# A decoder layer at one sequence of 256 tokens on one NeuronCore: four loads of x, modulation four k tiles ahead, later multiplies by the norm factor, and x1 scaled before it is transposed

## The chip, the cores and the metric

The kernel runs on one core of a Trainium2 chip. The metric is the device time of one execution in microseconds (us). The core has five engines that run side by side, each through its own instructions in its own order: PE (matrix products; PEld in the profile is its weight load), DVE (element-wise work), ACT (activation functions, with a scale and a bias per partition), POOL (hardly used here) and SP (issues most of the DMA transfers). An instruction that needs something from another engine or from a transfer waits at a semaphore, and everything queued behind it on its own engine waits with it.

## What is computed

One layer of a conditioned decoder, all in float32, for 256 tokens of 2048 channels:

```python
mod = silu(c) @ w_ada + b_ada        # shift1, scale1, gate1, shift2, scale2, gate2
h   = rms_norm(x, g_norm1) * (1 + scale1) + shift1
p   = h @ w_in                       # retention and HGRN2 inputs, and two branch gates
...                                  # yA, yB: the two attention-like branches
x   = x + gate1 * ((sigmoid(gA) * yA + sigmoid(gB) * yB) @ w_out)
h2  = rms_norm(x, g_norm2) * (1 + scale2) + shift2
u   = causal_depthwise_conv3(h2 @ w_up)
a, b = split(u)
x   = x + gate2 * ((silu(a) * b) @ w_down)
out = rms_norm(x, g_final)
```

The two places that the change touches are the two norms with their modulation: the one of x at the very start, and the one of x1 (x after the first branch) ahead of the product with w_up, called "up" below.

## The kernel before

**Products.** Every weight is read once, in pieces of 512 KB (128 partitions by 1024 float32 values, two k tiles of 128 rows by 512 columns). A float32 product is made of three products of rounded parts: ACT copies a piece to a rounded high part `wh` (line 165), DVE subtracts that from the piece to give the low part `wl` (line 170), and PE multiplies high by high, high by low and low by high (lines 187 to 189 with tokens as output rows, 200 to 202 and 913/915 with channels as output rows). There are 12 buffers for raw pieces and 4 each for `wh` and `wl`. The activations are split in the same way into the two halves of a tile (`hT` for the first norm, `h2T` for the second).

**Vectors of the conditioning.** The shift, scale and gate vectors come from w_ada by dot products on DVE (line 380, 1.2 us each, four per k tile of a scale and shift pair).

**The start.** `norm_x` loads x transposed (`xT`, four tiles of four k tiles each) in eight DMAs, squares each half tile (two on DVE, six on ACT), and adds the squares on DVE. `token_rstd` lets PE sum them over the partitions (line 290, 24 instruction records) and spreads the norm factor of each token over all partitions, `rx`. DVE multiplies x by it (`times`, line 370): the first two k tiles one by one from PSUM, and the other fourteen in seven multiplies of two k tiles from a copy `rx_sb`, which a dependence only holds behind the first weight split. `modulated` then writes the high part of `hT` and a full copy `h` on ACT (lines 341, 342), and DVE subtracts (343). Four output groups g = 0 to 3 are started with the first two k tiles; the next groups (g = 4, 5, 6, ...) follow, and a pacing helper interleaves the further dot products. A group's result is copied out of PSUM by ACT (line 691, tiles `p`).

**The x1 to up boundary.** x1 is kept with tokens on the partitions (tiles `xr`, four of 512 channels). The last quarter of the w_out product holds its last k tiles back so that the two token halves t = 0, 1 end apart. For each t, DVE forms gate times product and adds it to x1 (lines 879, 880), ACT squares and sums (882), and ACT and DVE make the norm factor `r` and from it a diagonal matrix `diag` (842). `turn_rows` (line 350) multiplies x1 by `diag` on PE, which transposes and scales it in one step, into a PSUM tile `po` that holds a pair of k tiles. `modulated2` turns each such pair into an `h2T` tile: ACT writes the high part of k tile 0 (line 359), a full copy `h` of k tile 0 (363) and the high part of k tile 1 (359); DVE makes the full copy of k tile 1 from PSUM (361); then DVE makes both low parts (365). `act2(k)` calls this two k tiles ahead of the product that is written next. Three pairs are transposed ahead of the first up product; the pairs 3 to 7 are transposed between up products. One piece of w_up is split ahead of the residual of the last quarter.

**Order.** In this stretch `pin` keeps every engine in the order in which the code is written. Elsewhere it is free where `self.ordered` is false, apart from the manual dependences.

## Time and profile before

| | |
|---|---|
| median of 3 runs | 1540.42 us (1540.33 to 1541.73) |
| the profiled execution | 1540.23 us |
| its span, first to last instruction | 1538.3 us |
| busy: PE, PEld | 1516.6 us (99%), 1308.0 us (85%) |
| busy: DVE, ACT | 1173.4 us (76%), 843.4 us (55%) |
| mean granted TensorE clock | 0.999 |
| read from HBM | 382.11 MB, 250 GB/s over the span |

The rows of a timeline give the start, the duration from first start to last end, the engine, the line, the operation, output and input tiles, and in brackets how long the engine was idle before it and what ended that. An instruction's duration includes a tail that overlaps the next one on the same engine: successive starts on ACT and DVE are some 0.1 us closer than the durations say. Most float32 products on PE have durations of about 0.4 us and start 0.23 us apart. The waits view adds up such idle times by the line that waited and the line that ended the wait.

### The profile page before, as it was taken

The numbers are of one execution on the slowest core, as the hardware profiler recorded it, in microseconds if no ns is written. First come the engines' busy times: TensorE is split into PE (matmuls) and PEld (weight loads), VectorE is DVE, ScalarE is ACT, GpSimd is POOL, SyncE is SP. The second block draws the span as 40 slices with busy tenths as digits, with TensorE's granted clock in tenths as the row PEclk, the third lists the DMA queues.
The fourth block names the chain that finished last, engine by engine and source line by source line (L and its number), as shares of the span: only waits on it lengthen the run. The fifth ranks groups of instructions, "written<-read, shape, count | busy, mean of one in ns | idle before, by whom it ended". The sixth has DMA issues, their size and how long they took to land.

```text
span 1538.3 us, 22200 instructions
## 1 busy us (share of the span) xinstructions
PE 1516.6 (99%) x8286; PEld 1308.0 (85%) x8286; DVE 1173.4 (76%) x1595; ACT 843.4 (55%) x1201; POOL 4.0 (0%) x8
## 2 busy tenths in 40 slices
PE   7999999999999999999999999999999999999997
PEld 6999999888888888888878888888888888888886
DVE  7899986897998977898757787777778769455454
ACT  5755454766865554445446555555555558444343
POOL 0000000000000000000000000000000000000000
PEclk9999999999999999999999999999999999999999
DMA  9999997687777789989946777777777766677651
GB/s 362 346 345 329 319 330 228 232 280 256 247 246 261 262 293 322 320 303 342 337 121 216 226 232 233 240 222 239 230 231 232 226 189 190 206 207 206 198 166 55
DMA packets 111568, 385.69 MB, mean 251 GB/s; under 512 B 12866, under 2 KB 13410, under 8 KB 111460
## 3 DMA queue, kind: packets, MB, share of 16 engines
q1 hardware_dynamic: 110592, 383.14, 76.0%
q8 instruction: 65, 1.06, 0.3%
q10 hardware_dynamic: 868, 1.13, 0.2%
q14 instruction: 43, 0.35, 0.1%
HBM read 382.11 MB, written 2.11 MB: 250 GB/s over the span
## 4 chain that ended last, share of the span: by engine, by line
PE 94%; DVE 3%; ACT 2%; DMA 1%; issue 1%; DVEq 0%; ACTq 0%
PE pg L188 13%; PE pg L187 13%; PE pg L189 13%; PE po L913 11%; PE pg L913 10%; PE po L915 5%; PE pg L915 5%; PE po L189 3%; PE po L188 3%; PE po L187 3%; PE pg L202 3%; PE pg L200 3%; PE pg L201 3%; PE po L556 1%; DVE raw L380 1%; PE po L200 1%
## 5 line engine op out<-in xcount | busy, mean ns | idle before, releaser
L170 DVE TENSOR_TENSOR wl<-raw,wh 128x1024 fp32r<-128x1024 f32 (+1 forms) x536 | 635.0, 1189 | 283.3 <-ACT wh L165 281.9
L165 ACT ACTIVATE wh<-raw 128x1024 fp32r<-128x1024 f32 (+1 forms) x536 | 550.9, 1033 | 529.9 <-PE pg L189 190.4
L380 DVE SCALAR_TENSOR_TENSOR raw<-raw,sc 128x1024 f32<-128x1024 f32 x192 | 233.2, 1217 | 0.0
L913 PE MATMUL pg<-h2T,wh 128*128 128x512 f32 x704 | 221.6, 396 | 1.7 <-DVE h2T L365 1.7
L913 PE MATMUL po<-h2T,wh 128*128 128x512 f32 x704 | 221.2, 395 | 0.2 <-ACT wh L165 0.2
L187 PE MATMUL pg<-wh,hT 128*128 128x512 f32 x512 | 202.6, 396 | 0.0
L188 PE MATMUL pg<-wl,hT 128*128 128x512 f32 x512 | 200.2, 391 | 0.7 <-DVE wl L170 0.7
L189 PE MATMUL pg<-wh,hT 128*128 128x512 f32 x512 | 199.8, 390 | 0.0
L915 PEld LDWEIGHTS pg<-h2T,wl 128*128 128x128 f32 x704 | 131.9, 188 | 31.7 <-DVE wl L170 0.8
L915 PEld LDWEIGHTS po<-h2T,wl 128*128 128x128 f32 x704 | 132.2, 188 | 31.1
L915 PE MATMUL pg<-h2T,wl 128*128 128x256 f32 x704 | 138.5, 278 | 0.0
L915 PE MATMUL po<-h2T,wl 128*128 128x256 f32 x704 | 138.3, 278 | 0.0
L188 PEld LDWEIGHTS pg<-wl,hT 128*128 128x128 f32 x512 | 96.3, 188 | 21.1 <-DVE wl L170 2.3
L189 PEld LDWEIGHTS pg<-wh,hT 128*128 128x128 f32 x512 | 96.1, 188 | 20.2
L187 PEld LDWEIGHTS pg<-wh,hT 128*128 128x128 f32 x512 | 96.2, 188 | 19.1
L202 PE MATMUL pg<-hT,wl 128*128 128x256 f32 x384 | 109.0, 284 | 0.8 <-DVE wl L170 0.8
L200 PE MATMUL pg<-hT,wh 128*128 128x256 f32 x384 | 109.3, 285 | 0.1
L201 PE MATMUL pg<-hT,wh 128*128 128x256 f32 x384 | 109.0, 284 | 0.0
L913 PEld LDWEIGHTS pg<-h2T,wh 128*128 128x128 f32 x704 | 107.2, 189 | 1.8 <-ACT h L363 1.8
L913 PEld LDWEIGHTS po<-h2T,wh 128*128 128x128 f32 x704 | 107.2, 189 | 0.7 <-ACT wh L165 0.6
L200 PEld LDWEIGHTS pg<-hT,wh 128*128 128x128 f32 x384 | 74.1, 193 | 0.9 <-ACT wh L165 0.6
L202 PEld LDWEIGHTS pg<-hT,wl 128*128 128x128 f32 x384 | 74.0, 193 | 1.0 <-DVE wl L170 1.0
(222 smaller groups left out, 2198.4 us busy)
## 6 DMA issues: line engine op xcount, KB each, us to landing
raw<-in_wup SPq DMA_DIRECT2D x176, 512.0 KB, 4.5
raw<-in_wdown SPq DMA_DIRECT2D x88, 512.0 KB, 3.6
raw<-in_wa SPq DMA_DIRECT2D x80, 512.0 KB, 5.6
raw<-in_ada SPq DMA_DIRECT2D x64, 512.5 KB, 5.6
raw<-in_ada SPq DMA_DIRECT2D x64, 512.0 KB, 5.7
raw<-in_wab SPq DMA_DIRECT2D x64, 512.0 KB, 4.8
raw<-in_gate SPq DMA_DIRECT2D x32, 512.5 KB, 4.9
raw<-in_wb SPq DMA_DIRECT2D x32, 512.0 KB, 5.2
```

Source lines behind the costliest of these rows:

```text
L165: self.pin(self.nc.scalar.activation(wh, raw, AF.Copy))
L170: self.last = self.nc.vector.tensor_tensor(wl, raw, wh.bitcast(F32), ALU.subtract)
L187: nc.tensor.matmul(ps[t], lhsT=hi, rhs=wh, start=first, stop=False)
L188: nc.tensor.matmul(ps[t], lhsT=hi, rhs=wl, start=False, stop=False)
L189: nc.tensor.matmul(ps[t], lhsT=lo, rhs=wh, start=False, stop=last)
L200: nc.tensor.matmul(out, lhsT=wh[:, cs], rhs=hi, start=opens, stop=False, skip_group_check=True)
L201: nc.tensor.matmul(out, lhsT=wh[:, cs], rhs=lo, start=False, stop=False, skip_group_check=True)
L202: nc.tensor.matmul(out, lhsT=wl[:, cs], rhs=hi, start=False, stop=last, skip_group_check=True)
L380: dot = self.pin(nc.vector.scalar_tensor_tensor(raw[:, 0, :], raw[:, 0, :], 1.0, self.sc[:, u * GW : u * GW + w], ALU.mult, ALU.mult, accu ...
L556: nc.tensor.matmul(ps[:, j * 64 : (j + 1) * 64], lhsT=(kt if n > 1 else k)[:, h, c * P : (c + 1) * P], rhs=eq[:, j * 64 : (j + 1) * 64], s ...
L913: self.pin(nc.tensor.matmul(ps[j + z], lhsT=wh[:, cs[z]], rhs=act, start=kt == 0, stop=False))
L915: nc.tensor.matmul(ps[j + z][:, :T], lhsT=wl[:, cs[z]], rhs=act[:, :T], start=False, stop=kt == KT - 1)
```

## The change

At the start, x is loaded in four DMAs, each tile is squared at once (one on DVE, three on ACT), the sums are folded to one k tile's width ahead of PE, and the multiplies of later k tiles by `rx_sb` move from "just after the first weight split" to the front of the generator of their own k tiles, held behind the weight split that was traced last. `modulated` makes the full copy of k tile 0 on DVE. At the boundary, `act2` works four k tiles ahead where it worked two, two pieces of w_up are split ahead of the residual where there was one, `modulated2` makes the full copy of the first k tile on DVE and of the second on ACT, with each low part right behind its full copy, and the pairs 3 to 7 are no longer transposed by a product with `diag`: `turn_scaled` multiplies x1 by the norm factor on DVE with tokens on the partitions (tile `xs`) and lets PE transpose that.

```diff
--- before.py
+++ after.py
@@ -268,9 +268,8 @@
     def load_x(self):
 
         out = [self.blk([P, 4, T], name="xT") for _ in range(4)]
-        for i in range(8):
-            u = slice(i % 2 * 2, i % 2 * 2 + 2)
-            self.pin(self.nc.sync.dma_start(out=out[i // 2][:, u, :], in_=self.a["xT"][:, 2 * i : 2 * i + 2, :]))
+        for i, z in enumerate(out):
+            self.pin(self.nc.sync.dma_start(out=z, in_=self.a["xT"][:, 4 * i : 4 * i + 4, :]))
         return out
 
     def load_rows(self, j):
@@ -314,23 +313,19 @@
         nc = self.nc
         self.xT = self.load_x()
         parts = []
-        for i in range(8):
-            x = self.xT[i // 2][:, i % 2 * 2 : i % 2 * 2 + 2, :]
-            z = self.s2([P, 2, T], name="sq")
-            if i < 2:
-                nc.vector.tensor_tensor(z, x, x, ALU.mult)
+        for i, x in enumerate(self.xT):
+            z = self.blk([P, 4, T], name="sq")
+            if i == 0:
+                self.pin(nc.vector.tensor_tensor(z, x, x, ALU.mult))
             else:
-                if self.silu:
+                if i < 3:
                     self.pin(nc.scalar.activation(*self.silu.pop(0), AF.Silu))
                 self.pin(nc.scalar.activation(z, x, AF.Square))
-            if i % 2:
-                nc.vector.tensor_tensor(z, z, last, ALU.add)
-                if i % 4 == 3:
-                    nc.vector.tensor_tensor(z[:, 0, :], z[:, 0, :], z[:, 1, :], ALU.add)
-                    parts.append(z[:, 0, :])
-                else:
-                    parts += [z[:, 0, :], z[:, 1, :]]
-            last = z
+            self.pin(nc.vector.tensor_tensor(z[:, :2, :], z[:, :2, :], z[:, 2:, :], ALU.add))
+            self.pin(nc.vector.tensor_tensor(z[:, 0, :], z[:, 0, :], z[:, 1, :], ALU.add))
+            parts.append(z[:, 0, :])
+        for part in self.silu:
+            self.pin(nc.scalar.activation(*part, AF.Silu))
         self.sqrt_table()
         return parts
 
@@ -339,7 +334,10 @@
         act = self.nc.scalar.activation
         h = self.s1([P, T], name="h")
         self.pin(act(dst[:, :T], x, AF.Identity, bias=sh[:, k : k + 1], scale=sc[:, k : k + 1]))
-        self.pin(act(h, x, AF.Identity, bias=sh[:, k : k + 1], scale=sc[:, k : k + 1]))
+        if k == 0:
+            self.pin(self.nc.vector.tensor_scalar(h, x, sc[:, k : k + 1], sh[:, k : k + 1], ALU.mult, ALU.add))
+        else:
+            self.pin(act(h, x, AF.Identity, bias=sh[:, k : k + 1], scale=sc[:, k : k + 1]))
         self.pin(self.nc.vector.tensor_tensor(dst[:, T:], h, dst[:, :T].bitcast(F32), ALU.subtract))
 
     def turn_rows(self, ps, x, k, diag, t):
@@ -348,6 +346,16 @@
             cols = slice((k + i) % 4 * P, ((k + i) % 4 + 1) * P)
             at = slice((NT * i + t) * P, (NT * i + t + 1) * P)
             self.pin(self.nc.tensor.matmul(ps[:, at], lhsT=x[k // 4][:, t, cols], rhs=diag[:, t, :], start=True, stop=True))
+
+    def turn_scaled(self, ps, x, rs):
+
+        z = self.s2([P, NT, 2 * P], name="xs")
+        for t in range(NT):
+            self.pin(self.nc.vector.tensor_scalar(z[:, t, :], x[:, t, :], rs[t], None, ALU.mult))
+        for t in range(NT):
+            for i in range(2):
+                at = slice((NT * i + t) * P, (NT * i + t + 1) * P)
+                self.pin(self.nc.tensor.transpose(ps[:, at], z[:, t, i * P : (i + 1) * P], self.ident))
 
     def modulated2(self, dst, ps, k, sc, sh):
 
@@ -358,10 +366,9 @@
             j = k + i
             self.pin(nc.scalar.activation(dst[:, i, :T], z[:, i, :], AF.Identity, bias=sh[:, j : j + 1], scale=sc[:, j : j + 1]))
             if i:
+                self.pin(nc.scalar.activation(h, z[:, i, :], AF.Identity, bias=sh[:, j : j + 1], scale=sc[:, j : j + 1]))
+            else:
                 self.pin(nc.vector.tensor_scalar(h, z[:, i, :], sc[:, j : j + 1], sh[:, j : j + 1], ALU.mult, ALU.add))
-            else:
-                self.pin(nc.scalar.activation(h, z[:, i, :], AF.Identity, bias=sh[:, j : j + 1], scale=sc[:, j : j + 1]))
-        for i, h in enumerate(hs):
             self.pin(nc.vector.tensor_tensor(dst[:, i, T:], h, dst[:, i, :T].bitcast(F32), ALU.subtract))
 
     def times(self, k, n, r):
@@ -671,12 +678,12 @@
             return hT[k // 2][:, k % 2, :]
 
         def ada1(k):
+            if k > 0 and k % 2 == 0:
+                ins = self.times(k, 2, rx_sb)
+                self.tc.add_manual_dep(ins.ins, self.last.ins.name, NOSYNC, reason="behind the weights traced ahead of it")
             yield from self.scale_shift("ada1", k, s1, t1, self.gn1)
             if k % 2 == 0:
                 hT[k // 2] = self.blk([P, 2, 2 * T], F32R, name="hT")
-                if k:
-                    ins = self.times(k, 2, rx_sb)
-                    self.tc.add_manual_dep(ins.ins, start.ins.name, NOSYNC, reason="after the start")
             self.modulated(act(k), self.xT[k // 4][:, k % 4, :], k, s1, t1)
             yield 0.7
 
@@ -694,23 +701,23 @@
 
 
         ada = [ada1(k) for k in range(KT)]
-        for _ in range(2):
+        for _ in range(3):
             next(ada[0])
         rx = self.token_rstd(parts)
         rx_sb = c.tile([P, T], F32, name="rx_sb")
         ps = [self.po2(), self.po2(), self.pg(), self.pg()][:FIRST]
         for k in range(2):
-            for i in range(4 if k else 2):
-                if i == 1:
+            for i in range(4 if k else 1):
+                if k and i == 1:
                     self.times(k, 1, rx)
                 next(ada[k])
+            if k == 0:
+                self.times(k, 1, rx)
             part = self.upper(a["wa"][0][:, k : k + 1, :], 1, G)
             for _ in ada[k]:
                 pass
             for g in range(FIRST):
                 wh, wl = self.rest(part if g == 0 else self.upper(a["wa"][g][:, k : k + 1, :], 1, G))
-                if k == 0:
-                    start = self.last
                 if k == g == 0:
                     self.pin(nc.scalar.activation(rx_sb, rx, AF.Copy))
                 mms[g](ps[g], act(k), wh[:, 0, :], wl[:, 0, :], k == 0, k == 1 and g >= RESIDENT)
@@ -831,14 +838,16 @@
             if last:
                 self.finish(ada2)
                 up = self.pieces(a["wup"][0], KT)
-                up = chain([next(up)], up)
+                up = chain([next(up), next(up)], up)
                 self.ordered = True
             if last:
                 diag = self.s1([P, NT, P], name="diag")
+                rs = []
             for t in range(NT):
                 self.residual(x1[j], ps, g, ss, j, t)
                 if last:
                     r = self.row_rstd(ss, part, t)
+                    rs.append(r)
                     self.pin(nc.vector.tensor_scalar(diag[:, t, :], self.ident, r, None, ALU.mult))
             if j == 2:
                 part = self.row_part(ss)
@@ -851,12 +860,11 @@
 
         def act2(k):
 
-            while len(h2T) < KT // 2 and 2 * len(h2T) <= k + 2:
+            while len(h2T) < KT // 2 and 2 * len(h2T) <= k + 4:
                 j = len(h2T)
                 if j >= len(turned):
                     turned.append(self.po())
-                    for t in range(NT):
-                        self.turn_rows(turned[j], x1, 2 * j, diag, t)
+                    self.turn_scaled(turned[j], x1[j // 2][:, :, j % 2 * 2 * P : (j % 2 + 1) * 2 * P], rs)
                 h2T.append(self.blk([P, 2, 2 * T], F32R, name="h2T"))
                 self.modulated2(h2T[j], turned[j], 2 * j, self.sc2, self.sh2)
             return h2T[k // 2][:, k % 2, :]
```

Line numbers of the changed kernel differ: 367, 369, 371 and 372 are the ACT parts, the DVE copy and the low parts of `modulated2`, 348 and 358 the two kinds of transposition, 354 the scaling, 921 and 923 the up products, 698 the copy out of PSUM, and 336 and 340 the ACT parts of `modulated`.

On DVE, at the boundary, right after the second `diag`, the kernel before has these instructions (h2T_7390, h2T_7399 and h2T_7430 are the pairs 0, 1 and 2, h2T_7466 is pair 3):

```order
L361 TENSOR_SCALAR h_7392<-po_7372,sc_137,sh_138 128x256
L365 TENSOR_TENSOR h2T_7390<-h_7391,h2T_7390 128x256
L365 TENSOR_TENSOR h2T_7390<-h_7392,h2T_7390 128x256
L361 TENSOR_SCALAR h_7401<-po_7373,sc_137,sh_138 128x256
L365 TENSOR_TENSOR h2T_7399<-h_7400,h2T_7399 128x256
L365 TENSOR_TENSOR h2T_7399<-h_7401,h2T_7399 128x256
L170 TENSOR_TENSOR wl_7427<-raw_7424,wh_7426 128x1024
L361 TENSOR_SCALAR h_7432<-po_7374,sc_137,sh_138 128x256
L365 TENSOR_TENSOR h2T_7430<-h_7431,h2T_7430 128x256
L365 TENSOR_TENSOR h2T_7430<-h_7432,h2T_7430 128x256
L170 TENSOR_TENSOR wl_7458<-raw_7455,wh_7457 128x1024
L361 TENSOR_SCALAR h_7468<-po_7461,sc_137,sh_138 128x256
```

The changed kernel has at the same place, from the third pair on (h2T_7400 is pair 2, h2T_7433 pair 3, h2T_7472 pair 4; xs_7426 and xs_7465 are the scaled x1 of pairs 3 and 4, wl_7461 is the third piece of w_up):

```order
L371 TENSOR_SCALAR h_7401<-po_7366,sc_127,sh_128 128x256
L372 TENSOR_TENSOR h2T_7400<-h_7401,h2T_7400 128x256
L372 TENSOR_TENSOR h2T_7400<-h_7402,h2T_7400 128x256
L354 TENSOR_SCALAR xs_7426<-xr_6817,rr_7351 128x256
L354 TENSOR_SCALAR xs_7426<-xr_6817,rr_7360 128x256
L371 TENSOR_SCALAR h_7434<-po_7425,sc_127,sh_128 128x256
L372 TENSOR_TENSOR h2T_7433<-h_7434,h2T_7433 128x256
L372 TENSOR_TENSOR h2T_7433<-h_7435,h2T_7433 128x256
L170 TENSOR_TENSOR wl_7461<-raw_7458,wh_7460 128x1024
L354 TENSOR_SCALAR xs_7465<-xr_6999,rr_7351 128x256
L354 TENSOR_SCALAR xs_7465<-xr_6999,rr_7360 128x256
L371 TENSOR_SCALAR h_7473<-po_7464,sc_127,sh_128 128x256
```

The scalings of a pair stand behind the low parts of the pair before and, from pair 4 on, behind the split of a piece of w_up; before, DVE had nothing to do for a transposition but `diag`.

On PE, around the transposition of pair 3, the kernel before has (h2T_7399 is pair 1, h2T_7430 pair 2):

```order
L913 MATMUL pg_7389<-h2T_7399,wh_7426 128x512 x2
L915 MATMUL pg_7389<-h2T_7399,wl_7427 128x256 x2
L350 MATMUL po_7461<-diag_7353,xr_6831 128x128 x4
L913 MATMUL pg_7388<-h2T_7430,wh_7457 128x512 x2
L915 MATMUL pg_7388<-h2T_7430,wl_7458 128x256 x2
L913 MATMUL pg_7389<-h2T_7430,wh_7457 128x512 x2
```

The changed kernel has (h2T_7382 is pair 0, h2T_7391 pair 1):

```order
L921 MATMUL pg_7381<-h2T_7382,wh_7335 128x512 x2
L923 MATMUL pg_7381<-h2T_7382,wl_7336 128x256 x2
L358 MATMUL po_7425<-ident,xs_7426 128x128 x4
L921 MATMUL pg_7380<-h2T_7391,wh_7341 128x512 x2
L923 MATMUL pg_7380<-h2T_7391,wl_7342 128x256 x2
L921 MATMUL pg_7381<-h2T_7391,wh_7341 128x512 x2
```

The transposition of pair 3 has moved from behind the k tiles 2 and 3 to behind the k tiles 0 and 1, and it reads `xs`, which DVE writes, where it read `xr` and `diag`.

On ACT, around the copies out of PSUM of the first groups behind the start, the kernel before has (p_143 and p_144 are the groups 4 and 5, wh_435 is the first weight piece of group 6, hT_426 the activation pair of the k tiles 2 and 3):

```order
L691 ACTIVATE p_143<-pg_369 128x1024
L391 ACTIVATE s_135<-dot_388 128x1
L392 ACTIVATE s_135<-gn_85,s_135 128x1
L165 ACTIVATE wh_435<-raw_433 128x1024
L691 ACTIVATE p_144<-pg_393 128x1024
L394 ACTIVATE t_136<-dot_418 128x1
L165 ACTIVATE wh_465<-raw_463 128x512
L341 ACTIVATE hT_426<-xT_95,t_136,s_135 128x256
L342 ACTIVATE h_428<-xT_95,t_136,s_135 128x256
```

The changed kernel has (p_133 and p_134 are the groups 4 and 5, wh_421 is the first piece of group 6, hT_413 the same activation pair):

```order
L698 ACTIVATE p_133<-pg_355 128x1024
L398 ACTIVATE s_125<-dot_375 128x1
L399 ACTIVATE s_125<-gn_85,s_125 128x1
L401 ACTIVATE t_126<-dot_405 128x1
L698 ACTIVATE p_134<-pg_380 128x1024
L336 ACTIVATE hT_413<-xT_95,t_126,s_125 128x256
L340 ACTIVATE h_414<-xT_95,t_126,s_125 128x256
L165 ACTIVATE wh_421<-raw_419 128x1024
L165 ACTIVATE wh_451<-raw_449 128x512
```

The first weight copy of group 6 has moved from ahead of the copy of group 5 to behind it and behind the two activations of the next k tile.

## The prediction

> **What bounds the kernel now.** I read the page's busy times first, then the waits of PE, then a table by stages, and only then the timelines of the two stages that the change touches.
>
> ```profile
> span 1538.3 us, 22200 instructions
> PE 1516.6 (99%) x8286; PEld 1308.0 (85%) x8286; DVE 1173.4 (76%) x1595; ACT 843.4 (55%) x1201; POOL 4.0 (0%) x8
> ```
>
> PE is busy for all but 21.7 us of the span. A faster DVE or ACT is worth nothing where PE has work, so the change can gain only where PE waits, and it can lose wherever it makes PE wait. The waits view of PE (what waited for what, us in total, times, longest) says where that is now:
>
> ```profile
> PE po L200 <- ACT hT L341: 3.5, 2, 2.6
> PE pg L913 <- DVE h2T L365: 1.7, 1, 1.7
> PE po L350 <- DVE diag L842: 1.3, 1, 1.3
> PE pg L202 <- DVE wl L170: 0.8, 1, 0.8
> ```
>
> L200 and L202 belong to the start, L350 and L913 to the x1 to up boundary. The table by stages (stage, its length, busy time of PE, PEld, DVE, ACT, POOL) places them:
>
> ```profile
> 0.00:50.00 50.00, 41.29 (x213) 34.16 (x214) 38.31 (x69) 30.04 (x51) 0.20 (x4) 1.00 0.99 371
> 100.00:200.00 100.00, 99.96 (x709) 94.10 (x708) 94.00 (x127) 53.20 (x77) 1.91 (x2) 1.00 0.97 332
> 200.00:300.00 100.00, 99.44 (x706) 93.51 (x705) 79.64 (x96) 58.77 (x76) 0.00 (x0) 1.00 0.75 252
> 780.00:796.00 16.00, 12.58 (x68) 10.42 (x67) 7.29 (x16) 6.91 (x16) 0.00 (x0) 1.00 0.24 71
> 796.00:820.00 24.00, 23.82 (x150) 20.54 (x149) 15.28 (x26) 15.66 (x26) 0.00 (x0) 1.00 0.45 132
> ```
>
> PE lacks 8.7 us in the first 50, 3.4 us from 780 to 796, and only 0.2 us from 796 to 820, where the pairs 3 to 7 are transposed and modulated now. That last row is the one to watch: the change rebuilds a stage that has nothing to gain.
>
> **The boundary: what starts earlier.** The timelines of PE, ACT and DVE around the first up product (start, duration, engine, line):
>
> ```profile
> 791.09 1.60 PE L350 MATMUL po<-diag,xr 128*128 128x128 f32 x12 [1.30 <-DVE diag L842]
> 794.37 0.70 PE L913 MATMUL pg<-h2T,wh 128*128 128x512 f32 x2 [1.68 <-DVE h2T L365]
> ```
>
> ```profile
> 791.84 0.56 ACT L359 ACTIVATE h2T<-po,sh,sc 128x256 fp32r<-128x256 f32 x1 [1.32 <-PE po L350]
> 792.30 0.55 ACT L363 ACTIVATE h<-po,sh,sc 128x256 f32<-128x256 f32 x1
> 792.75 1.02 ACT L359 ACTIVATE h2T<-po,sh,sc 128x256 fp32r<-128x256 f32 x2
> ```
>
> ```profile
> 793.35 0.54 DVE L361 TENSOR_SCALAR h<-po,sc,sh 128x256 f32<-128x256 f32 x1 [2.31 <-ACT h2T L359]
> 793.81 0.75 DVE L365 TENSOR_TENSOR h2T<-h,h2T 128x256 fp32r<-128x256 f32 x2
> ```
>
> DVE's copy at 793.35 reads only the PSUM tile that PE had finished before 791.84, yet it waited for ACT's read of it to end (two reads from 792.75, 0.45 apart: the first ends at 793.31). So ACT and DVE read one PSUM tile one after the other, in written order. In the changed kernel DVE's copy follows ACT's first read: it starts at 791.84 + 0.56 + 0.04 = 792.44 where it started at 793.35, and L913 comes as long behind it as now (794.37 - 793.35 = 1.02), at 793.46. That is 0.9 us earlier.
>
> **The boundary: what comes in its place.** The same order rule now holds inside each pair: ACT's high part of k tile 0, DVE's copy, ACT's high part and copy of k tile 1, one behind the other. Successive starts on ACT are 0.45 apart (792.30 to 792.75), so DVE's copy recurs in the next pair after 0.54 + 0.04 + 0.45 + 0.45 + 0.56 + 0.04 = 2.08 us: 792.44, 794.52, 796.60 for the pairs 0 to 2. The copy of k tile 1 of pair 2 ends on ACT at 796.60 + 0.58 + 0.45 + 0.55 + 0.04 = 798.22, its low part takes DVE some 0.34 more (0.75 for two), and only then, by the order of DVE, come the two scalings of pair 3. Scalings of this shape do not occur at the boundary now; the nearest rows are one multiply of the same size by a column (line 434) and the four transposes of another place, with the product behind them:
>
> ```profile
> L434 DVE TENSOR_SCALAR ang<-ang,freq x1: 350/350/350, 129.3 to 129.3; 128x256 f32<-128x256 f32 x1
> ```
>
> ```profile
> 669.36 0.60 PE L469 MATMUL po<-ident,gt 128*128 128x128 f32 x4
> 669.71 0.48 PE L187 MATMUL pg<-wh,og 128*128 128x512 f32 x1
> ```
>
> With 0.35 for a scaling (0.27 until the next starts), `xs` of pair 3 is complete at 798.56 + 0.27 + 0.35 = 799.18. The transposes of one token half start when that half's scaling is done, so two are left behind it, about half of 0.60 and of the 0.44 of PE (0.35 and the product's slow start). The k tiles 0 and 1 end by now at 793.46 + 2 x 1.39 = 796.24 (1.39: a quarter of the 5.65 from 794.37 to 800.02, below, without the 0.09 by which 669.71 shows a product behind a transposition to start slower, 0.32 for 0.23). PE stands in front of `xs` from 796.24 to 799.2, and k tile 2 starts at about 799.45.
>
> That would be a single loss, but it repeats. The transposition of pair 4 stands on PE ahead of k tile 4, its scaling on DVE stands behind the weight split of that k tile, the split waits for ACT's copy of the piece, and that copy stands on ACT behind the modulation of pair 3, which waits for the transposition of pair 3. With the two rows that price a weight piece (mean ns of one after the bar),
>
> ```profile
> L170 DVE TENSOR_TENSOR wl<-raw,wh 128x1024 fp32r<-128x1024 f32 x504 | 614.7, 1221 | 277.7 <-ACT wh L165 277.0
> L165 ACT ACTIVATE wh<-raw 128x1024 fp32r<-128x1024 f32 x504 | 532.2, 1060 | 523.7 <-PE pg L189 188.4 <-PE po L913 73.6 <-PE pg L913 70.3
> ```
>
> one turn of the circle is: last two transposes 0.36 + 0.03, high part 0.56 + 0.04, DVE copy 0.54 + 0.04, high part and copy of k tile 1 0.45 + 0.45 until ACT is free, weight copy 1.06 + 0.03, weight split 1.15 until the next start (1.22 less the 0.07 of overlap), scalings 0.27 + 0.35 + 0.05: 5.4 us. The kernel before does a pair in less, as PE's rows show:
>
> ```profile
> 800.02 1.06 PE L350 MATMUL po<-diag,xr 128*128 128x128 f32 x8
> 803.70 1.05 PE L350 MATMUL po<-diag,xr 128*128 128x128 f32 x8
> 814.88 1.06 PE L350 MATMUL po<-diag,xr 128*128 128x128 f32 x8
> 815.70 0.47 PE L913 MATMUL pg<-h2T,wh 128*128 128x512 f32 x1
> ```
>
> Its five transpositions come 3.72 us apart (14.86 for four), which is two k tiles (2.78) and a transposition. PE is never late there, because `diag` lies ready: nothing in that circle needs DVE. By the changed order k tile 4 starts at 804.8, 6 at 810.2, 8 at 815.6 and 10 at 821.0. Then there is no pair left to transpose, and k tile 12 needs only its weights: their copy starts 2.5 us behind the last two transposes (at 820.8), ends at 824.3 where the k tiles 10 and 11 end at 823.8, and the low part comes at 825.6, 0.8 us late for its first product. As if undisturbed, k tile 12 starts at 825.1. It starts at 815.7 now (and loses 0.2 at 819.4): **+9.2 us**, with the 0.9 gained taken in. As a list: 5.4 against 3.72 four times (6.7); 3.2 in front of pair 3, less the 0.9 that its transposition takes now (2.3); 1.3 at k tile 12 (0.5 for the high part, 0.8 for the low); less 0.9 and 0.2. Bounds: if the DVE copy did not hold up ACT's second read, the turn is 0.58 shorter and the boundary costs 6.6; with the durations not overlapping at all (0.1 more on each of nine steps) it is 0.9 longer, 12.8. The second early piece of w_up costs nothing: it is split before the residual begins, in DVE and ACT time that ended 3.1 and 5.8 us idle before it:
>
> ```profile
> 785.09 0.69 DVE L879 TENSOR_TENSOR gp<-po,g 128x512 f32<-128x512 f32 x1 [3.12 <-PE po L189]
> 786.54 0.63 ACT L882 ACTIVATE sq<-xr 128x512 bf16<-128x512 f32 x1 [5.83 <-DVE xr L880]
> ```
>
> **A clock rule weighed.** PE waits 1.30 and then 1.68 us around the last 12 records of L350 at the boundary now, and the products behind 794.37 still start 0.23 us apart: the clock stayed up. The changed circle leaves PE without products for about 2.6 us in each turn. The Trainium skill, "TensorE: Matmul & The Clock Gate" (Part 1), says that one idle window of about 3.4 us brings half clock, and in Part 4 that transposes do not count as busy. By that rule 2.6 us is still short of a window, and my sum stays; were it crossed, the sum would be that of the rival below.
>
> **The start.** The chain of waits goes through the sums of squares, and the DVE timeline and its group show the multiplies that stand ahead of the low part of k tile 1:
>
> ```profile
> 12.63 0.70 DVE sq L327
> 13.35 0.43 DVE sq L329
> ```
>
> ```profile
> L325 ACT ACTIVATE sq<-xT 128x512 f32<-128x512 f32 x6 | 3.6, 624 | 2.5 <-DMA xT<-in_xT 1.9 <-PE po L290 0.7
> ```
>
> ```profile
> 29.39 1.28 DVE L370 TENSOR_TENSOR xT<-xT,rx_sb 128x512 f32<-128x512 f32 x2
> 30.59 0.41 DVE L343 TENSOR_TENSOR hT<-h,hT 128x256 fp32r<-128x256 f32 x1
> L370 DVE TENSOR_TENSOR xT<-xT,rx_sb 128x512 f32<-128x512 f32 x7 | 4.5, 679 | 0.0
> ```
>
> The two adds stay; the square ahead of them is no longer held by PE's reading of an older one (0.7 us of waits on ACT, line 325), so the sums end 0.5 to 0.9 earlier. Four of the multiplies stand ahead of 30.59 now, 2.4 us at 0.60 a step, and go behind. K tile 1 and the groups behind it come up to 2.9 us earlier. But the gain must pass group 6:
>
> ```profile
> 41.74 0.39 PE L189 MATMUL pg<-wh,hT 128*128 128x512 f32 x1
> 43.33 0.39 PE L202 MATMUL pg<-hT,wl 128*128 128x256 f32 x1 [0.76 <-DVE wl L170]
> 40.98 1.04 ACT L165 ACTIVATE wh<-raw 128x1024 fp32r<-128x1024 f32 x1
> 42.16 1.02 ACT L691 ACTIVATE p<-pg 128x1024 f32<-128x1024 f32 x1
> 43.79 0.59 ACT L341 ACTIVATE hT<-xT,t,s 128x256 fp32r<-128x256 f32 x1
> ```
>
> Group 5 ends with 41.74, 2.9 us earlier at about 39.15. Its copy (42.16) now stands on ACT ahead of the weight copy of group 6 (40.98) and so do two activations of 0.5 a step: 39.2 + 0.93 + 1.0 puts that weight copy at about 41.2 to 42.25, its low part to 43.5, and L202 at 43.6 where it is 43.33. Net **+0.3**; between -1.2 (if the copy and the two activations take 1.5 less behind group 5) and +1.0 (k tile 1 gains only 2). The other six multiplies (0.6 to 0.68 each) go into 45 to 260 us, where DVE is busy 94 of 100 us and PE waits 0.04 (row 100 to 200): PE's lead hides them, since the same multiplies were done ahead before. If that cover is gone they cost up to 6 x 0.6 = 3.6.
>
> **Sum.** 9.2 + 0.3 = 9.5 on the profiled execution's 1540.23 us (span and 1.9 around it), which is 0.2 below the median of the runs: 1549.8, with the 0.2 about 1550.
>
> **The rivals.**
> Faster: the lookahead does what a lookahead should, and `xs` is ready whenever PE comes to it. It decides at a turn of 3.3 us (2.78 and the 0.44 of four transposes): below that PE is the bound again, each pair is 0.4 to 0.5 cheaper than with `diag` (five times, 2.3), 0.9 is kept and the start gives 1.2 at most: 1536. Against it stands that the copy, split and PSUM reads of the turn alone add to 4.3 us by rows. Chance 0.07.
> No change: the turn is some 3.7, so that only pair 3 and k tile 12 are waited for: 2.3 + 1.3 - 1.1 = 2.5, and the start 0.3: 1543. Chance 0.06.
> Cold clock: the rows do not show half clock after 1.7 us of waiting, and the turn waits longer. Were the products of the k tiles 2 to 11 at twice their time, a turn is 5.6 for them and 0.9 for transposes, 6.5 in place of 5.4 (four times 1.1), and 2.8 for k tiles 10 and 11: +7, 1557. Chance 0.07.
> DVE as the bound of the ada stretch: +3.6, 1553.6, inside the range. Chance 0.05.
> The forecast, with its bounds of 6.6 to 12.8 and -1.2 to +1.0: 0.75.
>
> **How the numbers follow.** The forecast's own range is 1545.5 to 1554.5; it reaches to 1556 for the cases above it, and the range of 8 in 10 is 1544.5 to 1556. A difference of 0.2% (3.1 us) is what a measurement of this kernel can tell from none. All cases but the first two are slower: 0.07, 0.06, 0.87.
>
> **What would show it.** In the profile after: the up product's first L921 near 793.5; PE waiting for `xs` (line 354) five times, some 3 us first and 2 to 2.6 then, with k tile pairs 5.4 apart until about 821; waits of L921 and L923 for the weights at k tile 12. At the start, the first products 1 to 2 us earlier, and a wait of some 3 us for the weight copy of group 6. I am wrong if PE's waits for line 354 sum to less than 4 us, or if the start keeps more than 2 us beyond group 6.

## The result, and the profile after

The changed kernel takes 1551.7 us (median of 6 runs, 1549.72 to 1553.73), the kernel before 1540.85 us (6 runs, 1540.25 to 1541.73): 1.0069 times, with a 95% interval of 1.0059 to 1.008, so 10.9 us slower. The forecast was 1550.0, slower, with 1544.5 to 1556. The profiled execution took 1550.3 us. One of the ten executions of the first run below took 3311.66 us, twice the others, and is left out of its comparison.

The page of the profile after, and its waits of PE:

```profile
span 1548.5 us, 22143 instructions
PE 1517.1 (98%) x8258; PEld 1308.2 (84%) x8258; DVE 1179.8 (76%) x1607; ACT 845.4 (55%) x1197; POOL 4.0 (0%) x8
```

```profile
PE po L358 <- DVE xs L354: 9.1, 5, 2.4
PE pg L200 <- ACT wh L165: 3.0, 1, 3.0
PE po L200 <- ACT hT L336: 1.6, 2, 1.2
PE pg L921 <- DVE h2T L372: 0.9, 1, 0.9
PE pg L202 <- DVE wl L170: 0.8, 1, 0.8
```

PE's work has not grown. The first two lines are new: PE stands five times, 9.1 us in all, in front of a scaling on DVE, and once, 3.0 us, in front of a weight copy. The waits for `hT` at the start (3.5 before) and for the first up product (1.7 before) have become 1.6 and 0.9. The stage that had nothing to gain shows the loss; it lacked 0.2 us of PE's work before and lacks 8 now:

```profile
796.00:820.00 24.00, 16.03 (x85) 13.28 (x83) 13.71 (x28) 11.85 (x20) 0.00 (x0) 0.93 0.23 66
```

To split a run at the boundary, take the row of PE that holds the first transposition by `diag` (line 350 before, 348 after, 12 records). Before it began at 788.21, with 1538.3 - 788.21 = 750.09 us behind it:

```profile
788.21 1.58 PE L350 MATMUL po<-diag,xr 128*128 128x128 f32 x12 [0.44 <-PE po L189]
```

After:

```profile
788.31 1.57 PE L348 MATMUL po<-diag,xr 128*128 128x128 f32 x12 [0.44 <-PE po L189]
793.69 0.70 PE L921 MATMUL pg<-h2T,wh 128*128 128x512 f32 x2 [0.89 <-DVE h2T L372]
799.10 0.70 PE L358 MATMUL po<-ident,xs 128*128 128x128 f32 x4 [2.39 <-DVE xs L354]
804.66 0.63 PE L358 MATMUL po<-ident,xs 128*128 128x128 f32 x4 [2.06 <-DVE xs L354]
810.14 0.63 PE L358 MATMUL po<-ident,xs 128*128 128x128 f32 x4 [2.06 <-DVE xs L354]
```

It begins 0.1 us later, and 1548.5 - 788.31 = 760.19 us follow: 10.1 of the profiled execution's 10.2 us are lost behind it. This second number, "from the first `diag` product to the end", is used for each experiment below, since it leaves out what varies from execution to execution at the start. In the five kernels here with the old boundary (the kernel before, and the runs below that change the start alone) it lies between 750.04 and 750.29.

One turn of the circle on DVE, from one scaling to the next:

```profile
804.16 0.61 DVE L354 TENSOR_SCALAR xs<-xr,rr 128x256 f32<-128x256 f32 x2
805.92 0.54 DVE L371 TENSOR_SCALAR h<-po,sc,sh 128x256 f32<-128x256 f32 x1 [1.15 <-ACT h2T L367]
806.50 0.42 DVE L372 TENSOR_TENSOR h2T<-h,h2T 128x256 fp32r<-128x256 f32 x1
807.56 0.43 DVE L372 TENSOR_TENSOR h2T<-h,h2T 128x256 fp32r<-128x256 f32 x1 [0.63 <-ACT h L369]
808.50 1.23 DVE L170 TENSOR_TENSOR wl<-raw,wh 128x1024 fp32r<-128x1024 f32 x1 [0.52 <-ACT wh L165]
809.65 0.61 DVE L354 TENSOR_SCALAR xs<-xr,rr 128x256 f32<-128x256 f32 x2
```

The brackets are the circle: DVE waits 1.15 us for ACT's first read, 0.63 for ACT's copy and 0.52 for ACT's weight copy, and PE then waits for DVE's scaling. A turn is 809.65 - 804.16 = 5.49 us, the forecast 5.4.

At the start, ACT's rows show the new order around group 6:

```profile
38.20 1.02 ACT L698 ACTIVATE p<-pg 128x1024 f32<-128x1024 f32 x1
39.12 0.59 ACT L336 ACTIVATE hT<-xT,t,s 128x256 fp32r<-128x256 f32 x1
39.62 0.59 ACT L340 ACTIVATE h<-xT,t,s 128x256 f32<-128x256 f32 x1
40.11 3.03 ACT L165 ACTIVATE wh<-raw 128x1024 fp32r<-128x1024 f32 x4
```

The copy of group 5 comes 3.96 us earlier than before (42.16), the weight copy of group 6 only 0.87 earlier (40.98).

### The profile page after: what moved, and what is told of

Read it like the earlier page. It is cut to its first block, busy times and chain, and to the rows that moved or that the text cites. A ratio compares the mean times of both kernels' runs of the same rounds, so it can differ in the third digit from the quotient of the medians.

```text
span 1548.5 us, 22143 instructions
## 1 busy us (share of the span) xinstructions
PE 1517.1 (98%) x8258; PEld 1308.2 (84%) x8258; DVE 1179.8 (76%) x1607; ACT 845.4 (55%) x1197; POOL 4.0 (0%) x8
## 4 chain that ended last, share of the span: by engine, by line
PE 92%; DVE 3%; ACT 3%; DMA 1%; issue 1%; SPq 0%; DVEq 0%; ACTq 0%
PE pg L188 13%; PE pg L187 13%; PE pg L189 13%; PE po L921 11%; PE pg L921 10%; PE po L923 5%; PE pg L923 5%; PE pg L202 3%; PE pg L200 3%; PE pg L201 3%; PE po L188 3%; PE po L187 3%; PE po L189 3%; DVE wl L170 1%; PE po L201 1%; PE po L202 1%
## 5 line engine op out<-in xcount | busy, mean ns | idle before, releaser
L202 PE MATMUL pg<-hT,wl 128*128 128x256 f32 x384 | 109.7, 286 | 0.8 <-DVE wl L170 0.8
L202 PEld LDWEIGHTS pg<-hT,wl 128*128 128x128 f32 x384 | 74.7, 194 | 1.0 <-DVE wl L170 1.0
```

Of the source, the lines that this page charges most:

```text
L202: nc.tensor.matmul(out, lhsT=wl[:, cs], rhs=hi, start=False, stop=last, skip_group_check=True)
```

## The experiments

The theory is the prediction's: the boundary loses because the transposition waits for a scaling that stands on DVE behind a weight split, in a circle; the start gains and gives it back at group 6. In each of the three groups of runs the kernel before ran on the same chip: 1541.6, 1541.48 and 1541.44 us. "D" below is the time from the first `diag` product to the end of the profiled execution, less 750.09. Each D comes from one trace; the five kernels with the old boundary differ by 0.25 us. Line numbers shift from run to run: 345 to 362 hold the two kinds of transposition, 908 to 937 the up products.

**The start alone.** The change without its boundary:

```diff
-                up = chain([next(up), next(up)], up)
+                up = chain([next(up)], up)
-            while len(h2T) < KT // 2 and 2 * len(h2T) <= k + 4:
+            while len(h2T) < KT // 2 and 2 * len(h2T) <= k + 2:
-                    self.turn_scaled(...)
+                    for t in range(NT):
+                        self.turn_rows(turned[j], x1, 2 * j, diag, t)
...
```

(and `modulated2` as before.)

> The change's start with the boundary of the kernel before. Theory (the circle through DVE at the boundary makes the loss, the start nets nothing): the trace of the changed kernel is 0.1 us late where the last held product of the w_out stage starts (787.49 against 787.38), so 1540.9, between 1540.2 and 1542.0, with one wait of about 3 us of PE for the weight copy of group 6. Rival (the start is what makes the kernel slower, by what it does to the stages behind it): over 1545.

Measured: 1540.52 against 1541.6 (0.9995, 0.9985 to 1.0005): no difference clear of noise, D = +0.1, and the wait of group 6 is there:

```profile
PE pg L200 <- ACT wh L165: 3.0, 1, 3.0
```

The start isn't what makes the change slower.

**`diag` for all pairs.** The changed kernel, with the scaling and its transposition undone:

```diff
-                    self.turn_scaled(turned[j], x1[j // 2][:, :, j % 2 * 2 * P : (j % 2 + 1) * 2 * P], rs)
+                    for t in range(NT):
+                        self.turn_rows(turned[j], x1, 2 * j, diag, t)
...
```

> The changed kernel, but the pairs 3 to 7 are transposed and scaled by the product with diag as before; four k tiles ahead, the new order in modulated2 and the second early piece of w_up are kept. Theory (the circle exists only because the transposition waits for a scaling on DVE that stands behind the weight split): no wait of PE for DVE between the k tiles 0 and 11 beyond 1 us, first up product at 793.7, 1540.2, between 1539.3 and 1541.5. Rival (the order within modulated2 or the lookahead itself makes the loss, since both put one engine behind the other): 1546 or more. Rival (the clock that drops is the price): half clock seen again after 810 and over 1543.

Measured: 1542.88 against 1541.6 (1.0012, 1.0002 to 1.0021), D = 1542.9 - 790.82 - 750.09 = +2.0. Of the 10.1 us at the boundary 8.1 go with the scaling, so the circle is the main cost. But the rest of the boundary isn't a gain of 0.8; it loses 2.0, which puts the time outside the 1539.3 to 1541.5 of the theory, with waits of PE for the weights in place of those for `xs`:

```profile
PE pg L912 <- DVE wl L170: 1.4, 3, 0.5
PE pg L910 <- DVE h2T L362: 0.9, 1, 0.9
PE pg L910 <- ACT wh L165: 0.4, 1, 0.4
```

So the first rival of that run was right about a part. At the boundary the clock stays at 1.00 in this run, so half clock isn't what loses them.

**Scaling one pair earlier.** The changed kernel, with the scaling issued behind the low parts of the pair before, ahead of the weight split:

```diff
+                n = 3 if j == 0 else j + 1
+                if n < KT // 2 and (j == 0 or j > 2):
+                    xs[n] = self.scaled(x1[n // 2][:, :, n % 2 * 2 * P : (n % 2 + 1) * 2 * P], rs)
...
```

> The changed kernel, but each scaling of x1 is issued one pair earlier on DVE, right behind the low parts of the pair before it and so ahead of the weight split. Theory: the turn of the circle loses the weight copy and the split (2.2 us less the tail, 3.6 in place of 5.5), which is no more than a pair takes with diag (3.72); left are a wait of about 2 us for the second scaled pair and 1.3 at k tile 12, so 1542.4, between 1541 and 1544. Rival (transposing after a scaling is dear as such): 1547 or more.

Measured: 1542.72 (1.0012, 1.0002 to 1.0022), D = 1540.9 - 787.75 - 750.09 = +3.1. Moving two instructions per pair ahead of the weight split, with the same work, takes 7 of the 10.1 us away; that a transposition after a scaling is dear as such is excluded. What is left of the waits for scalings is two instead of five:

```profile
PE po L362 <- DVE xs L354: 2.0, 2, 1.7
```

The rest is not waits for scalings alone: PE also waits 1.3 us, four times, for DVE's low part of the weights, and in this trace a stretch of half clock falls between the second and the third scaled pair (granted clock 0.53 from 803.00 to 806.40).

**The multiplies alone.** The kernel before with one part of the start:

```diff
         def ada1(k):
+            if k > 0 and k % 2 == 0:
+                ins = self.times(k, 2, rx_sb)
+                self.tc.add_manual_dep(ins.ins, self.last.ins.name, NOSYNC, ...)
             yield from self.scale_shift("ada1", k, s1, t1, self.gn1)
             if k % 2 == 0:
                 hT[k // 2] = self.blk([P, 2, 2 * T], F32R, name="hT")
-                if k:
-                    ins = self.times(k, 2, rx_sb)
-                    self.tc.add_manual_dep(ins.ins, start.ins.name, NOSYNC, ...)
```

> The kernel before with one thing changed: the multiplies of x by the norm factor are moved behind the weight splits as in the change. Theory (this move alone brings the low part of k tile 1 2.4 us earlier, and alone puts the weight copy of group 6 behind the copy of group 5, so that the gain is given back there): PE waits 2 to 3 us for that weight copy, and the time is 1541.0, between 1540.2 and 1542.5. Rival (the multiplies were simply in the way): 1538.6 or less.

Measured: 1543.47 (1.0016, 1.0007 to 1.0025): 1.9 us slower, more than the 0.2 that was expected, D = 0.0. The wait of group 6 is there, and the gain that should pay for it is small: k tile 1 begins at 29.20 where it began at 29.87.

```profile
29.68 0.42 DVE L343 TENSOR_TENSOR hT<-h,hT 128x256 fp32r<-128x256 f32 x1 [1.49 <-ACT h L342]
29.20 0.51 PE L200 MATMUL po<-hT,wh 128*128 128x256 f32 x2 [1.19 <-ACT hT L341]
30.16 0.50 PE L201 MATMUL po<-hT,wh 128*128 128x256 f32 x2 [0.45 <-DVE hT L343]
45.94 0.39 PE L200 MATMUL pg<-hT,wh 128*128 128x256 f32 x1 [3.03 <-ACT wh L165]
```

So the moved multiplies free less than the 2.4 us of the prediction: DVE's low part of k tile 1 starts 0.91 us earlier (29.68 for 30.59), since with the multiplies gone DVE waits 1.49 us for ACT's copy `h`. In this trace PE then ran at half clock, behind the waits of 1.19 and 0.45 us:

```profile
30.70:34.10 3.40, 3.40 (x18) 3.40 (x17) 2.17 (x5) 1.57 (x2) 0.00 (x0) 0.51 1.03 411
```

Group 5 so ended later than in the kernel before (its last product starts at 42.52 for 41.74), and the clock fell once more behind group 6 (0.54 from 47.60 to 51.00). This execution took 1544.92 us, 1.45 above the median; whether the others had the same stretches isn't shown.

**The loads and sums alone.** The kernel before with `load_x` and `norm_x` of the change:

```diff
-        for i in range(8):
-            u = slice(i % 2 * 2, i % 2 * 2 + 2)
-            self.pin(self.nc.sync.dma_start(out=out[i // 2][:, u, :], in_=self.a["xT"][:, 2 * i : 2 * i + 2, :]))
+        for i, z in enumerate(out):
+            self.pin(self.nc.sync.dma_start(out=z, in_=self.a["xT"][:, 4 * i : 4 * i + 4, :]))
...
```

> The kernel before with only the four loads of x, the squares of whole tiles and the shorter sums; the multiplies stay early and ACT's order around group 6 stays as before. Theory (the early part of the start gains, x lands 1.8 us earlier, and only the moved multiplies make ACT's order give it back): no wait of 3 us for the weight copy of group 6, and 2 us less than the kernel before, between 0.8 and 3 less. Rival (the stream of weights sets the end of the start, so that earlier sums buy nothing): within 0.5 us of it.

Measured: 1538.93 against 1541.48 (0.9984, 0.9975 to 0.9994): 2.5 us faster, with D = +0.1 and no wait of 3 us. Since D is no smaller than before, the gain is made ahead of the boundary.

**The whole start, with early multiplies.** The start alone, with the multiplies where they stood:

```diff
-            if k > 0 and k % 2 == 0:
-                ins = self.times(k, 2, rx_sb)
...
+                if k:
+                    ins = self.times(k, 2, rx_sb)
+                    self.tc.add_manual_dep(ins.ins, start.ins.name, NOSYNC, ...)
```

> The change's whole start with the boundary of the kernel before, but the multiplies of x stand where they stood, behind the first weight split only. It differs from the run of the start alone in the multiplies' place. Theory: the weight copy of group 6 stands ahead of the copy of group 5 again, so no wait of 3 us there, and 2 us less than the kernel before, between 0.8 and 3.5 less. Rival (the multiplies, early again, hold up k tile 1 by 2.4 us): as much as the start alone, 0 to 1 us less than the kernel before.

Measured: 1538.53 against 1541.48 (0.9985, 0.9975 to 0.9994): 2.9 us faster. Against the start alone (1.1 faster, in another group of runs) the late multiplies cost 1.9 us, as much as in the run with them alone. ACT's rows show the order:

```profile
38.17 1.03 ACT L689 ACTIVATE p<-pg 128x1024 f32<-128x1024 f32 x1 [0.95 <-PE pg L189]
39.09 0.28 ACT L392 ACTIVATE t<-dot 128x1 f32<-128x1 f32 x1
39.27 1.05 ACT L165 ACTIVATE wh<-raw 128x1024 fp32r<-128x1024 f32 x1
40.89 1.02 ACT L689 ACTIVATE p<-pg 128x1024 f32<-128x1024 f32 x1
```

The weight copy of group 6 (39.27) stands ahead of the copy of group 5 (40.89) again, and PE starts group 6 without a wait for it.

**The order in `modulated2` alone.** The kernel before with:

```diff
             if i:
+                self.pin(nc.scalar.activation(h, z[:, i, :], ...))
+            else:
                 self.pin(nc.vector.tensor_scalar(h, z[:, i, :], ...))
-            else:
-                self.pin(nc.scalar.activation(h, z[:, i, :], ...))
-        for i, h in enumerate(hs):
             self.pin(nc.vector.tensor_tensor(dst[:, i, T:], h, dst[:, i, :T].bitcast(F32), ALU.subtract))
```

> The kernel before with one thing changed: modulated2 in the order of the change (DVE's full copy of the first k tile right behind ACT's first read). Theory: the first up product starts 0.7 to 0.9 us earlier, the rest of the boundary stays bound by PE, so 0.8 us less than the kernel before, between 1.5 less and 0.2 less. Rival (ACT and DVE taking turns on one PSUM tile, with ACT idle 0.6 us per pair, brings waits for the weights): no gain, or up to 1.5 us more.

Measured: 1543.36 against 1541.48 (1.0014, 1.0005 to 1.0024), D = 1540.6 - 787.95 - 750.09 = +2.6. The theory fell; the rival held, and went further. The first up product gains its 0.8 (793.32 - 787.95 = 5.37 behind the first `diag` product, 6.16 before), and 3.4 are lost behind it, at the weights:

```profile
PE pg L914 <- DVE wl L170: 1.2, 3, 0.5
PE pg L912 <- ACT wh L165: 0.9, 2, 0.5
```

**Two k tiles ahead.** The run with `diag` for all pairs, and:

```diff
-            while len(h2T) < KT // 2 and 2 * len(h2T) <= k + 4:
+            while len(h2T) < KT // 2 and 2 * len(h2T) <= k + 2:
```

> The run with diag for all pairs, but two k tiles ahead instead of four; start, order in modulated2 and two early pieces as changed. Theory (what was left of the loss there, 2.0 us from the first diag product to the end against the kernel before, comes from weight copies that stand on ACT behind the modulation of a pair that is needed two k tiles later): from the first diag product to the end 749.3 us, 0.8 less than the kernel before (750.09), and 1.5 us less in all, between 0.5 and 3 less. Rival (the order in modulated2, or the second early piece, makes these 2.0): 751.5 or more.

Measured: 1541.57 against 1541.48 (1.0005, 0.9996 to 1.0015), D = 1539.1 - 787.83 - 750.09 = +1.2. The theory was not right, and the rival only in part: four k tiles ahead cost 0.8 (2.0 to 1.2), and the rest stays. At the boundary this run differs from the run of the new order alone only by the second early piece of w_up, so that piece does not cost but saves 1.4 (2.6 to 1.2), and the rest is the order's.

**The old order in the changed kernel.** Only `modulated2` undone:

> The changed kernel with one thing undone: the old order in modulated2, so that ACT makes its three reads of a pair without waiting for DVE. Theory (the circle's turn is the sum of its steps): the turn is 0.8 us shorter (ACT's three steps of 0.45 and the weight copy follow one another: 4.65 in place of 5.48), four turns and the tail make 3.5 to 4, less the 0.8 of the first product: 2.5 to 3.5 less than the changed kernel, 7.5 us more than the kernel before, between 6 and 9.5 more. Rival (the wait for xs is set by DVE's load alone): as slow as the changed kernel, 10 to 12 more.

Measured: 1546.1 against 1541.44 (1.0036, 1.0022 to 1.005), 4.7 us more than the kernel before, D = 1545.7 - 790.17 - 750.09 = +5.4. The turn is shorter:

```profile
804.58 0.63 PE L358 MATMUL po<-ident,xs 128*128 128x128 f32 x4 [1.52 <-DVE xs L354]
809.51 0.63 PE L358 MATMUL po<-ident,xs 128*128 128x128 f32 x4 [1.50 <-DVE xs L354]
```

4.93 in place of 5.48: 0.55, about the 0.58 that the prediction gave for DVE's copy holding up ACT, less than the 0.8 expected here. The total fell by more than expected (4.7 more than the kernel before, where 6 to 9.5 was the range), as the first wait for `xs` shrank too (2.39 to 0.22) and no half clock fell into the boundary (granted clock 1.00 from 795 to 825).

**The new order for pair 0 only.** The start with early multiplies, with two early pieces of w_up and

```diff
-            if i:
+            if i == (k > 0):
                 self.pin(nc.vector.tensor_scalar(h, z[:, i, :], ...))
+                if k == 0:
+                    self.pin(nc.vector.tensor_tensor(dst[:, i, T:], h, ...))
             else:
                 self.pin(nc.scalar.activation(h, z[:, i, :], ...))
...
```

> The run with the change's start and early multiplies (2.9 us less than the kernel before), plus two things at the boundary: the order of the change in modulated2 for pair 0 alone, the old order for all other pairs, and two early pieces of w_up; diag and two k tiles ahead as before. Theory (the new order gains 0.8 at the first up product and loses on every later pair by holding ACT): 3.7 us less than the kernel before, between 2.7 and 5 less, and no waits for weights between the k tiles 0 and 11. Rival (the 0.8 is given back at the next wait for weights): 2.9 less.

Measured: 1537.64 against 1541.44 (0.998, 0.9971 to 0.9989): 3.8 us faster than the kernel before, near the 3.7 that was expected. D = 1535.3 - 785.82 - 750.09 = -0.6. The first up product keeps the gain of the new order (791.19 - 785.82 = 5.37 behind the first `diag` product), and PE runs through the pairs without a wait, on its old period:

```profile
796.95 1.06 PE L348 MATMUL po<-diag,xr 128*128 128x128 f32 x8
800.63 1.05 PE L348 MATMUL po<-diag,xr 128*128 128x128 f32 x8
804.38 1.05 PE L348 MATMUL po<-diag,xr 128*128 128x128 f32 x8
```

**Scaled pairs, two pairs ahead.** That run, with the transposition of the change and

```diff
+                n = j + 2
+                if 3 <= n < KT // 2:
+                    xs[n] = self.scaled(x1[n // 2][:, :, n % 2 * 2 * P : (n % 2 + 1) * 2 * P], rs)
...
```

> The run just described, but the pairs 3 to 7 are scaled on DVE and transposed by PE as in the change, with the scaling issued two pairs ahead (behind the low parts of pair j - 2). Theory (the scaled transposition is cheaper on PE, 0.44 against 0.9 for four, and costs only where the transposition has to wait for the scaling): PE never waits for a scaling, a pair takes 3.2 to 3.4 us in place of 3.72, and 5.5 us less than the kernel before, between 4 and 7 less. Rival (DVE, with 3.0 us of work per pair, becomes what PE waits for): 3.7 less or worse, with waits for the weights' low part.

Measured: 1537.36 against 1541.44 (0.9976, 0.9967 to 0.9985), 4.1 us faster than the kernel before and not to be told from the run just above; D = 1537.7 - 788.49 - 750.09 = -0.9. PE never waits for a scaling, and the transposition is cheaper, but the weights take the gain:

```profile
799.62 0.60 PE L362 MATMUL po<-ident,xs 128*128 128x128 f32 x4
802.86 0.60 PE L362 MATMUL po<-ident,xs 128*128 128x128 f32 x4
804.69 0.51 PE L937 MATMUL pg<-h2T,wl 128*128 128x256 f32 x2 [0.76 <-DVE wl L170]
807.13 0.60 PE L362 MATMUL po<-ident,xs 128*128 128x128 f32 x4
```

3.24 us from the first to the second, as expected, but 4.27 to the third: behind two of the five transpositions PE waits some 0.76 us for DVE's split. The rival, DVE as the next limit, is what the rows show.

## Why the prediction was right, point by point

**The first up product.** Forecast at 793.46, 0.9 earlier; it came at 793.69 in a trace that was 0.1 late, so 0.8 earlier. The step that was too short is DVE's own: the low part started 0.58 behind the copy (792.54 to 793.12), not 0.46, because it needs that copy.

**The first wait.** `xs` of pair 3 was forecast complete at 799.18 and was at 799.31; k tile 2 began at 799.56 for 799.45. The wait itself was 2.39 us where some 3 was named: PE's records of the k tiles 0 and 1 end at 796.7, not at 796.24.

**The circle.** 5.4 forecast, 5.49 measured, and each step that the working names stands in the rows. Four runs show it as the cause and not as a description: without the scaling D falls from 10.1 to 2.0; with the scaling ahead of the split, to 3.1; two pairs ahead, in the better order, to -0.9; with one hold of 0.58 taken out, the turn falls by 0.55.

**The sum at the boundary.** 9.2 forecast, 10.1 measured. Four turns 0.09 longer are 0.4. Another part is the clock, which the forecast kept up. Three stretches of 3.4 us from the windows view (the third number from the end is the granted clock; they hold 13, 14 and 19 records of PE, where such stretches of the kernel before at full clock hold 21, from 795.20, and 30, from 43.60):

```profile
810.80:814.20 3.40, 3.40 (x13) 2.87 (x12) 1.61 (x4) 2.53 (x4) 0.00 (x0) 0.52 0.52 157
821.40:824.80 3.40, 3.40 (x14) 2.97 (x13) 1.35 (x3) 1.99 (x4) 0.00 (x0) 0.54 0.46 154
42.80:46.20 3.40, 3.40 (x19) 3.40 (x18) 3.40 (x6) 0.34 (x1) 0.00 (x0) 0.52 1.03 407
```

Half clock came after waits of 2.06 us. That is the rival of the cold clock, half true: the first stretch cost nothing, because PE would have waited for `xs` anyway (the wait that follows is 0.51 where the others are 2.06, and the turn is the same), the second delayed the last transposition's reader on ACT by 0.4 (2.76 us idle in front of it, 2.33 in the other turns). The Trainium skill, "TensorE: Matmul & The Clock Gate" (Part 1), gives a window of about 3.4 us for both directions. The length of the slow stretches agrees with it. That a gap of 2.6 us is still short of a window, as the prediction took from it, does not: a wait of 2.06 us, or 2.4 with the transposes, was enough twice.

Three waits of 2.06 us brought half clock twice, so the wait alone doesn't decide. What differs is how much of PE's work falls into the 3.41 us just before a slow stretch:

```profile
797.16:800.57 3.41, 1.47 (x9) 1.29 (x10) 1.61 (x6) 1.59 (x3) 0.00 (x0) 1.00 0.00 0
807.40:810.81 3.41, 1.35 (x9) 1.08 (x9) 2.18 (x4) 1.07 (x3) 0.00 (x0) 1.00 0.04 6
817.64:821.05 3.41, 1.40 (x9) 1.03 (x7) 2.26 (x5) 1.79 (x3) 0.00 (x0) 1.00 0.14 56
```

Half clock followed the second and the third of these, with 1.35 and 1.40 us of work, and not the first, with 1.47. So PE need not be idle throughout; where the limit lies, these runs don't show.

The last term of the sum, 1.3 us at k tile 12, did not come as the wait that the prediction named. The k tiles 10 and 11 ran partly at half clock and took 4.13 us (821.81 to 825.94) in place of 2.78, and behind that only a weight load waits, 0.52 us for the low part:

```profile
826.65 0.30 PEld L923 LDWEIGHTS pg<-h2T,wl 128*128 128x128 f32 x2 [0.52 <-DVE wl L170]
```

At full clock PE would have come to k tile 12 at about 824.3 (an estimate: 821.5 + 2.78), while ACT began to copy its piece at 824.28 and DVE to split it at 825.37, so the named wait would probably have stood there. That the term kept its size with another cause is luck.

**What the sum left out.** It took the new order in `modulated2` for a gain of 0.9 with a hold inside the circle, and the rest of it for free. The runs show that without the circle the order loses 2.6 at the boundary, four k tiles ahead another 0.8, and the second early piece is worth 1.4 there. In the changed kernel the turn of the circle already holds the order's 0.55, and PE's waits list no wait of an up product for weights, so the rest of these costs seems to hide behind the circle. Whether the early piece is worth nothing there, as the prediction put it, isn't shown: no run took it out of the changed kernel.

**The start.** Forecast +0.3, measured +0.1 at the first `diag` product, and -1.1 with an interval over 0 for the start alone. The mechanism held: the gain stops at group 6, 3.04 us of wait for about 3. Two terms were mis-sized. The loads and sums were put at 0.5 to 0.9 and are worth 2.5 alone. The multiplies were put at a gain of 2.4 that is given back; only 0.9 of it showed at k tile 1, and moving them costs 1.9. The two errors have opposite signs, so that the net came out near is partly luck. In the profiled run a third term was missing: behind that wait the clock fell to half from 42.8 to 46.2, and the 0.86 us by which L202 came earlier (42.47 for 43.33) were lost again.

**The signs that were named.** The waits for line 354 sum to 9.1 us, not less than 4, and the start keeps nothing beyond group 6. The first products came 2.8 us earlier (17.23 for 20.04), where 1 to 2 was named.

**What stays open.** The start's -1.1 and the boundary's 10.1 would make 1549.9, as in the fastest runs of the changed kernel (1549.72); the median is 1.8 higher. Their mean clock is 0.993 to 0.996 where the kernel before has 0.997 to 0.999 in the last group of runs, so half clock in other places or for longer is likely, but that isn't shown: only one execution has a trace.

## What to carry to other kernels

An operation that is moved from a lightly used path to a busy in-order engine must be priced with everything that stands ahead of it there, and with the question whether any of that waits, by way of other engines, for the operation's own result of the turn before: such a circle costs its whole length each turn, and here it was broken by issuing the operation earlier, with the same work. In these traces ACT and DVE read one PSUM tile one behind the other in written order (ACT stood idle 0.61 us for DVE's copy in each pair); whether the chip or the program's own dependences enforce that isn't shown. An order that shortens the first pass can then lengthen each later one; here it paid when it was used for the first pass only. When a gain at the start doesn't reach the end, look at the order of the copies on the engine that feeds the next group.

## What the runs showed of the hardware that was not expected

PE's clock fell to about half for 3.4 us after waits of 2.06 us with four transposes between, in two of the five places where PE waited for a scaling, and after waits of 3.04 and 0.76 us at the start. Four loads of twice the size brought the last of x earlier: at 8.88 us in the changed kernel, where eight ended at 10.72 in the kernel before. Over all traces here, four ended between 8.41 and 10.06 (ten traces) and eight between 9.77 and 11.12 (three), so the two overlap a little. Four transposes took PE 3.24 - 2.78 = 0.46 us per pair, four products with `diag` 0.9 (3.72 - 2.78).
